# Differential attention: both components' scores into one two-bank tile, one maximum for both, softmax statistics of four heads together

## The chip, the cores and the metric

One core of a Trainium2 chip runs the whole forward pass of a two-layer encoder trunk. The metric is the device time of one execution in microseconds (us); smaller is better. The kernel before takes 2676.36 us (median of three runs, 2675.62 to 2678.28).

## The reference, cut to what matters

Each layer has three head groups that read one input projection: RWKV-7, differential attention, and gated linear attention (GLA). Their outputs meet in one output projection; a mixture of 16 experts follows. The change is in the differential attention (4 heads, two components of 64 dimensions each per head, values of 128; 512 tokens behind 16 meta tokens, so L = 528):

```python
q = rotary(q...) * (B_QK_DIM ** -0.5)      # (B, 4 heads, 2 components, L, 64)
k = rotary(k...)                            # the same shape
def attend(qb):
    s = einsum("bhcqd,bhckd->bhcqk", qb, k)
    pr = softmax(s, axis=-1)                # each component by itself
    w = pr[:, :, 0] - lam * pr[:, :, 1]
    return einsum("bhqk,bhkv->bhqv", w, v)
o_meta = attend(q[:, :, :, :N_META])        # the 16 meta tokens
o_real = lax.map(attend, q_real)            # 4 blocks of 128 queries
o = rms_norm(concatenate(o_meta, o_real), subln_g) * (1.0 - lam_init)
```

## The kernel before

A layer goes through three stages. In the first, the 28 blocks of the input projection (`pj`, L297, float32 as sums of products of a high and a low part) run on TensorE (PE), and GLA and the chunks of the RWKV recurrence are laid between them. `heads` (L763) takes the twelve attention blocks of that projection: for every head it makes `q{h}` and `k{h}`, in which the partitions 0 to 63 hold component 0 and 64 to 127 component 1 (`hr(c)` is that half), after a rotation on VectorE (DVE) and GpSimd (POOL). `k{h}` is stored twice as wide as `q{h}`: a slice of it for each component, in which the other component's half is zero (memset on POOL), so that a product over all 128 rows with `q{h}` gives one component's scores.

In the second stage `attention` (L884) goes through query blocks of 128 in the order 1, 2, meta, 3, 4. For a block PE makes the scores against the 16 meta keys (tile `sm`, L897), ScalarE (ACT) copies them to `smeta` (L900), and DVE takes their maxima `mxm` (L901). Then, for each of four heads and two components: PE makes the scores of 128 queries by 512 keys in one PSUM bank (`S`, L907; `s_tile` has four banks); DVE takes the row maximum (L908) and turns it with `mxm` into the bias (L909); ACT makes the exponentials and their sums (L911), and the same of `smeta` (L913). Per head follow three small statistics on DVE (L915 to L917), the combination of both components (L918 for `e`, L919 for `em`), four transposes on PE into `pt` (L923), their copy `wt` (ACT L927 for heads 0 to 2, DVE L929 for head 3) and four products with the values into `po` (L931). After the heads come the meta weights (`pm`, `wm`, `vM`) and `norm` (L805): `o` and its square on ACT, about fifteen operations on DVE in a chain, four transposes `pf`, and `mxh`/`mxl`, the inputs of the output projection. The meta tokens go through `attend_meta` (L832), all heads in one tile. The last RWKV steps (L587 to L618) and the splitting of the output weights (`wo_h` on ACT L988, `wo_l` on DVE L989, eight each) are laid into this stage as well.

In the third stage the output projection (L1092) runs on PE. Its PSUM tiles take the place of the score tiles, so its first product waits until the last exponential has read its scores. Then the router and the experts follow.

The Tile scheduler fixes, when the kernel is built, the order of instructions on each engine; each engine runs its own list in order and waits where an operand is late. The few lines that matter most:

```python
for c in range(2):
    p = s_tile("S")
    behind(T.matmul(p[:R], qk[0, h][:, qo:qo + R], qk[1, h][:, c, NM:], start=True, stop=True), mark)
    V.tensor_reduce(s_[:, c:c + 1], p[:R], axis=AX.X, op=OP.max)
    V.tensor_scalar(s_[:, c:c + 1], s_[:, c:c + 1], mxm[:R, h, c:c + 1], -0.125, op0=OP.max, op1=OP.mult)
```

## Time and profile before

| | us |
|---|---|
| median of three runs | 2676.36 |
| the profiled execution, its own time | 2676.92 |
| its span in the trace | 2675.1 |
| PE busy | 2498.5 (93%) |
| DVE busy | 2121.9 (79%) |
| ACT busy | 1589.3 (59%) |
| POOL busy | 345.0 (13%) |
| mean granted TensorE clock, share of full speed | 0.951 |

The span goes from the first to the last instruction on the core; 1.8 us of the execution lie around it. Busy shares are means over stages with different limits: the experts take most of the span, and attention about 83 us in each layer. Layer 1's attention stage is from 436.7 us (the first copy of `smeta`) to 519.2 us, layer 2's from 1758 to 1842 us. A share in one of these windows tells about this stage; the shares above do not.

### The profile page before, as it was taken

The page shows a single profiled execution, that of the slowest core. Times are in us where ns is not written, and L with a number is a line of the kernel's source. Part 1 is how long each engine was busy: PE and PEld are TensorE (multiplying, and loading weights), DVE is VectorE, ACT ScalarE, POOL GpSimd, SP SyncE. Part 2 cuts the span into 40 slices and gives each one's busy share as a digit, 9 for nine tenths or more (in the row PEclk, how much of TensorE's full clock was granted, in tenths as well). Part 3 has the DMA queues.
Part 4 walks back from the last instruction along what each step waited for, and adds up shares of the span by engine and source line. Part 5 has one row for each costly group of instructions (what it writes and reads, how often), then busy time and mean ns, then how long its engine had stood idle before and what let it go on. Part 6 is the DMA issues. An engine that isn't in the chain of part 4 may idle for free. (4 is left out here: it accounts for less than half of the span.)

```text
span 2675.1 us, 54651 instructions
## 1 busy us (share of the span) xinstructions
PE 2498.5 (93%) x22106; PEld 2104.4 (79%) x22106; DVE 2121.9 (79%) x3645; ACT 1589.3 (59%) x2337; POOL 345.0 (13%) x503
## 2 busy tenths in 40 slices
PE   7898999897999999999888899999699999999995
PEld 6787876567888888888687787866489898988894
DVE  3557677858999999999735667777699999999995
ACT  4324334515878787888642343354177878787884
POOL 2212331000000000000121133210000000000000
PEclk9878999998999999999988889999899999999998
DMA  4101111158999999999620111012499999999994
GB/s 132 40 33 53 36 35 48 63 198 324 402 400 405 403 403 405 400 408 416 233 84 33 40 45 47 16 68 105 171 387 392 410 399 409 398 409 400 406 420 151
DMA packets 84717, 643.80 MB, mean 241 GB/s; under 512 B 12592, under 2 KB 13040, under 8 KB 35312
## 3 DMA queue, kind: packets, MB, share of 16 engines
q1 hardware_dynamic: 75936, 618.16, 57.8%
q0 software_dynamic: 8528, 22.15, 3.3%
q8 instruction: 173, 2.83, 0.4%
q14 instruction: 80, 0.66, 0.1%
HBM read 617.05 MB, written 19.40 MB: 238 GB/s over the span
## 5 line engine op out<-in xcount | busy, mean ns | idle before, releaser
L1162 DVE TENSOR_TENSOR wl<-w,wh 128x1280 fp32r<-128x1280 f32 (+2 forms) x896 | 1161.4, 1334 | 81.7 <-ACT wh L1161 58.6
L1161 ACT ACTIVATE wh<-w 128x1280 fp32r<-128x1280 f32 (+2 forms) x896 | 1008.4, 1149 | 200.9 <-PE h3b L1215 70.5
L1283 PE MATMUL py<-wh,hh 128*66 128x512 f32 (+1 forms) x768 | 288.6, 376 | 3.2 <-ACT hh L1263 3.2
L1283 PE MATMUL py<-wh,hl 128*66 128x512 f32 (+1 forms) x768 | 287.2, 374 | 0.0
L1283 PE MATMUL py<-wl,hh 128*66 128x512 f32 (+1 forms) x768 | 287.2, 374 | 0.0
L1215 PE MATMUL h1a<-wh,xx 128*66 128x256 f32 x1024 | 243.4, 296 | 0.0
L1215 PE MATMUL h3a<-wh,xx 128*66 128x256 f32 x1024 | 241.5, 294 | 0.0
L1288 POOL DMA_INDIRECT hbuf<-yo,idx x32 | 63.9, 1998 | 1188.2 <-ACT yo L1287 1078.1
L1215 PE MATMUL h1T<-xx,wh 128*128 128x132 f32 x768 | 175.8, 229 | 0.0
L1215 PE MATMUL h3T<-xx,wh 128*128 128x132 f32 x768 | 174.2, 227 | 0.0
L297 PE MATMUL pj<-uh,wh 128*128 128x264 f32 (+1 forms) x896 | 166.3, 314 | 5.4 <-ACT kS L353 5.0
L297 PE MATMUL pj<-ul,wh 128*128 128x264 f32 (+1 forms) x896 | 163.5, 315 | 0.0
L297 PE MATMUL pj<-uh,wl 128*128 128x264 f32 (+1 forms) x896 | 155.3, 303 | 0.0
L1283 PEld LDWEIGHTS py<-wh,hh 128*66 128x66 f32 x768 | 104.8, 136 | 60.9 <-ACT hh L1263 3.5
L1283 PEld LDWEIGHTS py<-wl,hh 128*66 128x66 f32 x768 | 104.7, 136 | 60.7
L1215 PE MATMUL h1a<-wl,xx 128*66 128x256 f32 x512 | 151.8, 296 | 0.0
L1215 PE MATMUL h3a<-wl,xx 128*66 128x256 f32 x512 | 151.1, 295 | 0.0
L1283 PEld LDWEIGHTS py<-wh,hl 128*66 128x66 f32 x768 | 104.8, 136 | 58.1 <-DVE hl L1264 0.7
L1215 PE MATMUL h1T<-xx,wl 128*128 128x66 f32 x768 | 150.1, 195 | 0.0
L1215 PE MATMUL h3T<-xx,wl 128*128 128x66 f32 x768 | 148.9, 194 | 0.0
L1215 PEld LDWEIGHTS h1T<-xx,wh 128*128 128x128 f32 x768 | 148.5, 193 | 0.0
L1215 PEld LDWEIGHTS h3T<-xx,wh 128*128 128x128 f32 x768 | 146.8, 191 | 0.0
(462 smaller groups left out, 6000.9 us busy)
## 6 DMA issues: line engine op xcount, KB each, us to landing
w<-in_e_w SPq DMA_DIRECT2D x384, 1408.0 KB, 15.8
w<-in_w_in SPq DMA_DIRECT2D x56, 512.0 KB, 3.3
wo<-in_w_out SPq DMA_DIRECT2D x16, 512.0 KB, 3.3
h<-hbuf SPq DMA_DIRECT2D x12, 512.0 KB, 5.1
swp<-raw SPq DMA_DIRECT2D x64, 66.0 KB, 2.0
h<-in_x SPq DMA_DIRECT2D x8, 512.0 KB, 7.0
hbuf<-h SPq DMA_DIRECT2D x8, 512.0 KB, 2.9
ubuf<-u POOLq DMA_DIRECT2D x8, 512.0 KB, 7.3
```

The source lines that it names most:

```text
L297: T.matmul(p[:M, c, :HL], ww[:, k, :M], uu[:, k, c * HL:(c + 1) * HL], start=(n == 0), stop=(n == 23))
L1161: A.activation(wh, w[:, lo:hi], AF.Copy)
L1162: sub = V.tensor_sub(wl, w[:, lo:hi], wh.bitcast(F32))
L1215: T.matmul(o_, l_, r_, start=s0, stop=s1)
L1283: T.matmul(py[:CAP, c, d0:d0 + n], x[:, kk, :], ww[:, at0 - lo:at0 - lo + n], start=(kk == 0 and i_ == 0), stop=(kk == FK - 1 and i_ == 2))
L1288: G.indirect_dma_start(out=hbuf[:, :], out_offset=bass.IndirectOffsetOnAxis(ap=idx[:CAP, e:e + 1], axis=0), in_=yo[:CAP], in_offset=None, ...
```

## The change

`k{h}` becomes as wide as `q{h}`: one addition over 128 partitions takes the place of two over 64, and eight zero fills go. A small tile `kM` holds the 16 meta keys of each head and component with zeros in the other half (one memset and eight copies of 64 x 16 on POOL). The scores of a component are a product over its own 64 rows; both components of a head go to the two banks of one tile (`s_tile`: two tiles of two banks, where there were four of one). One maximum over 128 x 2 x 512 and one small operation make both biases. `smeta` is copied with the factor -0.125, so that a minimum takes the place of the maximum. The statistics (sum, reciprocal, ratio, meta weights) are made once per block, for four heads at a time, behind the exponentials of all four heads; then come the four combinations of `e`. The fourth `wt` copy goes from DVE to ACT. In `attend_meta` one product takes the place of two that were added up.

```diff
-        return banks["pool"].tile([128, 512], F32, name=name, tag="s", bufs=4)
+        return banks["pool"].tile([128, 2, 512], F32, name=name, tag="s", bufs=2)
...
+            kM = at.tile([128, 4, 2, NM], F32, name="kM")
+            G.memset(kM, 0.0)
...
-                    if which == 0:
-                        q_ = at.tile([128, L], F32, name=f"q{h}")
-                        V.tensor_add(q_, raw, swp)
-                    else:
-                        q_ = at.tile([128, 2, L], F32, name=f"k{h}")
+                    q_ = at.tile([128, L], F32, name=f"{'qk'[which]}{h}")
+                    V.tensor_add(q_, raw, swp)
+                    if which == 1:
                         for c in range(2):
-                            G.memset(q_[hr(1 - c), c, :], 0.0)
-                            V.tensor_add(q_[hr(c), c, :], raw[hr(c)], swp[hr(c)])
+                            G.tensor_copy(kM[hr(c), h, c, :], q_[hr(c), :NM])
...
-            p, pe = s_tile("S"), s_tile("pe")
+            p2 = s_tile("S")
+            p, pe = p2[:, 0], p2[:, 1]
...
-                for c in range(2):
-                    mm(pe[r, :NM], buf[:, r], qk[1, h][:, c, :NM], start=(c == 0), stop=(c == 1),
-                       tile_position=(0, 32 * h))
-                for c in range(2):
-                    mm(p[r, :], buf[:, r], qk[1, h][:, c, NM:], start=(c == 0), stop=(c == 1),
-                       tile_position=(0, 32 * h))
+                mm(pe[r, :NM], buf[:, r], qk[1, h][:, :NM], start=True, stop=True, tile_position=(0, 32 * h))
+                mm(p[r, :], buf[:, r], qk[1, h][:, NM:], start=True, stop=True, tile_position=(0, 32 * h))
...
-                st = at.tile([128, 4, 12], F32, name="st", bufs=2)
                 e4 = em[qt % 2]
-                pe = s_tile("sm")[:, :128].rearrange("p (h c n) -> p h c n", h=4, c=2)
+                stat = lambda name: at.tile([128, 4, 2], F32, name=name, bufs=2)
+                pe = s_tile("sm")[:, 0, :128].rearrange("p (h c n) -> p h c n", h=4, c=2)
                 for h in range(4):
-                    behind(T.matmul(pe[:R, h], qk[0, h][:, qo:qo + R], qk[1, h][:, :, :NM], start=True, stop=True), mark)
+                    behind(T.matmul(pe[:R, h], qk[0, h][:, qo:qo + R], kM[:, h], start=True, stop=True), mark)
                 sm_ = at.tile([128, 4, 2, NM], F32, name="smeta", bufs=2)
-                mxm = at.tile([128, 4, 2], F32, name="mxm", bufs=2)
-                A.activation(sm_[:R], pe[:R], AF.Copy)
-                V.tensor_reduce(mxm[:R], sm_[:R], axis=AX.X, op=OP.max)
+                low, big_, sums, part, rec = (stat(n_) for n_ in ("low", "big", "sums", "part", "rec"))
+                A.activation(sm_[:R], pe[:R], AF.Copy, scale=-0.125)
+                V.tensor_reduce(low[:R], sm_[:R], axis=AX.X, op=OP.min)
+                es = []
                 for h in range(4):
-                    s_ = st[:R, h]
                     e = wp.tile([128, 1024], F32, name="e", tag=("w", "wh")[h % 2])[:R].rearrange("p (c n) -> p c n", c=2)
+                    p = s_tile("S")
                     for c in range(2):
-                        p = s_tile("S")
-                        behind(T.matmul(p[:R], qk[0, h][:, qo:qo + R], qk[1, h][:, c, NM:], start=True, stop=True), mark)
-                        V.tensor_reduce(s_[:, c:c + 1], p[:R], axis=AX.X, op=OP.max)
-                        V.tensor_scalar(s_[:, c:c + 1], s_[:, c:c + 1], mxm[:R, h, c:c + 1], -0.125,
-                                        op0=OP.max, op1=OP.mult)
-                        A.activation(e[:, c], p[:R], AF.Exp, scale=0.125, bias=s_[:, c:c + 1],
-                                     accum_out=s_[:, 2 + c:3 + c])
-                        A.activation(sm_[:R, h, c], sm_[:R, h, c], AF.Exp, scale=0.125, bias=s_[:, c:c + 1],
-                                     accum_out=s_[:, 8 + c:9 + c])
-                    V.tensor_add(s_[:, 2:4], s_[:, 2:4], s_[:, 8:10])
-                    V.reciprocal(s_[:, 4:6], s_[:, 2:4])
-                    V.scalar_tensor_tensor(s_[:, 6:7], s_[:, 5:6], nlam[:R], s_[:, 2:3], op0=OP.mult, op1=OP.mult)
-                    V.scalar_tensor_tensor(e[:, 0], e[:, 1], s_[:, 6:7], e[:, 0], op0=OP.mult, op1=OP.add)
-                    V.scalar_tensor_tensor(e4[:R, h, :NM], sm_[:R, h, 1], s_[:, 6:7], sm_[:R, h, 0],
-                                           op0=OP.mult, op1=OP.add)
+                        behind(T.matmul(p[:R, c], qk[0, h][hr(c), qo:qo + R], qk[1, h][hr(c), NM:],
+                                        start=True, stop=True), mark)
+                    V.tensor_reduce(big_[:R, h], p[:R], axis=AX.X, op=OP.max)
+                    V.scalar_tensor_tensor(big_[:R, h], big_[:R, h], -0.125, low[:R, h], op0=OP.mult, op1=OP.min)
+                    for c in range(2):
+                        A.activation(e[:, c], p[:R, c], AF.Exp, scale=0.125, bias=big_[:R, h, c:c + 1],
+                                     accum_out=sums[:R, h, c:c + 1])
+                        A.activation(sm_[:R, h, c], sm_[:R, h, c], AF.Exp, scale=-1.0, bias=big_[:R, h, c:c + 1],
+                                     accum_out=part[:R, h, c:c + 1])
+                    es.append(e)
+                V.tensor_add(sums[:R], sums[:R], part[:R])
+                V.reciprocal(rec[:R], sums[:R])
+                ratio = part[:R, :, 0]
+                V.scalar_tensor_tensor(ratio, rec[:R, :, 1], nlam[:R], sums[:R, :, 0], op0=OP.mult, op1=OP.mult)
+                V.tensor_mul(sm_[:R, :, 1], sm_[:R, :, 1], ratio[:, :, None].to_broadcast([R, 4, NM]))
+                V.tensor_add(e4[:R, :, :NM], sm_[:R, :, 1], sm_[:R, :, 0])
+                for h in range(4):
+                    e = es[h]
+                    V.scalar_tensor_tensor(e[:, 0], e[:, 1], part[:R, h, 0:1], e[:, 0], op0=OP.mult, op1=OP.add)
                     pt = sm_tile("pt")
                     for t in range(4):
                         T.transpose(pt[:, t * 128:t * 128 + R], e[:, 0, t * 128:(t + 1) * 128], ident[:R, :R])
                     wt = at.tile([128, 528], F32, name="wt", tag="tb", bufs=4)[:, :512].rearrange("p (t n) -> p t n", t=4)
                     pv4 = pt.rearrange("p (t c) -> p t c", t=4)[:, :, :R]
-                    if h < 3:
-                        A.activation(wt[:, :, :R], pv4, AF.Copy)
-                    else:
-                        V.tensor_copy(wt[:, :, :R], pv4)
+                    A.activation(wt[:, :, :R], pv4, AF.Copy)
...
-                norm(at, po, st[:R, :, 4], qo, R)
+                norm(at, po, rec[:R, :, 0], qo, R)
```

The two lists of instructions differ in three places as follows. Numbers behind a tile's name tell its instance; `x2` is two instructions in a row.

ACT, layer 1, end of block 1 (its last heads' exponentials, `e_5507` and `e_5536`) and the start of block 2 (`smeta_5607`, `e_5611`), before:

```order
L911 ACTIVATE e_5507,st_5439<-S_5514,st_5439 128x512
L913 ACTIVATE smeta_5445,st_5439<-smeta_5445,st_5439 128x16
L900 ACTIVATE smeta_5607<-sm_5602 128x128
L911 ACTIVATE e_5536,st_5439<-S_5537,st_5439 128x512
L617 ACTIVATE mxh_5224<-zf_5308 128x80
L927 ACTIVATE wt_5501<-pt_5496 128x512
...
L913 ACTIVATE smeta_5445,st_5439<-smeta_5445,st_5439 128x16
L911 ACTIVATE e_5536,st_5439<-S_5543,st_5439 128x512
L913 ACTIVATE smeta_5445,st_5439<-smeta_5445,st_5439 128x16
L927 ACTIVATE wt_5530<-pt_5525 128x512
L617 ACTIVATE mxh_5224<-zf_5344 128x128
L911 ACTIVATE e_5611,st_5601<-S_5612,st_5601 128x512
```

The same place after; `e_5480` is block 1's last head and `e_5592` block 2's first:

```order
L908 ACTIVATE e_5480,sums_5445<-S_5481,big_5444 128x512
L910 ACTIVATE smeta_5442,part_5446<-smeta_5442,big_5444 128x16
L896 ACTIVATE smeta_5584<-sm_5579 128x128
L617 ACTIVATE mxh_5222<-zf_5306 128x80
L596 ACTIVATE zf_5378<-Y_2114 128x128
L610 ACTIVATE zf_5342<-pg_5365 128x128
L927 ACTIVATE wt_5501<-pt_5496 128x512
L617 ACTIVATE mxh_5222<-zf_5342 128x128
L927 ACTIVATE wt_5513<-pt_5508 128x512
L610 ACTIVATE zf_5378<-pg_5401 128x128
...
L927 ACTIVATE wt_5537<-pt_5532 128x512
L908 ACTIVATE e_5592,sums_5587<-S_5593,big_5586 128x512
```

Before, the copies `wt` of block 1 stood among its exponentials; now all four stand behind the last of them and ahead of block 2's first.

DVE at the same place, before: the maximum of block 2's first scores (`S_5612`) stands ahead of the combination of block 1's last head (`e_5536`).

```order
L915 TENSOR_TENSOR st_5439<-st_5439 128x2
L908 TENSOR_REDUCE st_5601<-S_5612 128x1
L615 SCALAR_TENSOR_TENSOR zf_5344<-pf_5370,pv_72,zf_5344 128x128
L194 SCALAR_TENSOR_TENSOR rq_u_5388<-rq_u_5388,m2_5379 128x2
L916 RECIPROCAL st_5439<-st_5439 128x2
L909 TENSOR_SCALAR st_5601<-st_5601,mxm_5608 128x1
L195 SCALAR_TENSOR_TENSOR rq_y_5387<-rq_u_5388,rq_y_5387 128x2
L917 SCALAR_TENSOR_TENSOR st_5439<-st_5439,lam_88 128x1
L618 TENSOR_TENSOR mxl_5225<-zf_5344,mxh_5224 128x128
L196 TENSOR_TENSOR rq_u_5388<-rq_y_5387 128x2
L918 SCALAR_TENSOR_TENSOR e_5536<-e_5536,st_5439 128x512
```

After: the ratio (L916), the meta weights (L917, L918) and the four combinations of block 1 (`e_5450` to `e_5480`) stand ahead of block 2's first maximum (`big_5586`).

```order
L916 SCALAR_TENSOR_TENSOR part_5446<-rec_5447,lam_88,sums_5445 128x4
...
L917 TENSOR_TENSOR smeta_5442<-smeta_5442,part_5446 128x4x16
...
L918 TENSOR_TENSOR em1_4915<-smeta_5442 128x4x16
...
L921 SCALAR_TENSOR_TENSOR e_5450<-e_5450,part_5446 128x512
...
L921 SCALAR_TENSOR_TENSOR e_5460<-e_5460,part_5446 128x512
...
L921 SCALAR_TENSOR_TENSOR e_5470<-e_5470,part_5446 128x512
...
L921 SCALAR_TENSOR_TENSOR e_5480<-e_5480,part_5446 128x512
L618 TENSOR_TENSOR mxl_5223<-zf_5342,mxh_5222 128x128
L196 TENSOR_TENSOR rq_u_5386<-rq_y_5385 128x2
L905 TENSOR_REDUCE big_5586<-S_5593 128x2
...
L905 TENSOR_REDUCE big_5586<-S_5603 128x2
...
L906 SCALAR_TENSOR_TENSOR big_5586<-big_5586,low_5585 128x2 x2
```

Block 2's maxima moved behind everything that block 1's statistics have to do.

PE at the end of layer 1's attention, around the first product of the output projection (L1092), before:

```order
L923 MATMUL pt_6113<-cst_66,e_6095 128x128 x4
L1092 MATMUL po_6234<-wo_h_5421,mxh_5224 128x512 x2
L1092 MATMUL po_6234<-wo_h_5421,mxl_5225 128x512 x2
L931 MATMUL po_6026<-vB_4913,wt_6118 128x128 x4
L923 MATMUL pt_6142<-cst_66,e_6124 128x128
L825 MATMUL pf_6019<-cst_66,o_5996 128x128 x4
L923 MATMUL pt_6142<-cst_66,e_6124 128x128 x3
L1092 MATMUL po_6234<-wo_l_5422,mxh_5224 128x512 x2
L1092 MATMUL po_6234<-wo_h_5421,mxh_5224 128x512 x2
L931 MATMUL po_6026<-vB_4913,wt_6147 128x128 x4
L934 MATMUL pm_6153<-cst_66,em0_4916 128x128
...
L937 MATMUL po_6026<-vM_4914,wm_6155 128x512
```

After, where that line is L1090:

```order
L903 MATMUL S_6000<-k3_4907,q3_4637 128x512 x2
L1090 MATMUL po_6143<-wo_h_5419,mxh_5222 128x512 x2
L1090 MATMUL po_6143<-wo_h_5419,mxl_5223 128x512 x2
L824 MATMUL pf_5948<-cst_66,o_5925 128x128 x4
...
L924 MATMUL pt_6015<-cst_66,e_5969 128x128 x4
...
L932 MATMUL pm_6062<-cst_66,em0_4914 128x128
...
L929 MATMUL po_5955<-vB_4911,wt_6020 128x128 x4
L924 MATMUL pt_6027<-cst_66,e_5979 128x128 x4
L924 MATMUL pt_6039<-cst_66,e_5989 128x128 x4
...
L929 MATMUL po_5955<-vB_4911,wt_6032 128x128 x4
L929 MATMUL po_5955<-vB_4911,wt_6044 128x128 x4
L924 MATMUL pt_6051<-cst_66,e_5999 128x128 x4
```

Of block 4's transposes `pt` and value products `po` those of two heads stood ahead of the output projection's first product, and of a third head the transposes; now all four heads' stand behind it.

## Rows read from the trace of the kernel before

**Rows 1.** Windows: stretch, us, then busy us of PE, PEld, DVE, ACT, POOL, clock, DMA

```profile
436.70:519.20 82.50, 73.49 (x421) 43.98 (x421) 75.44 (x288) 56.58 (x181) 5.30 (x10) 0.98 0.16 57
...
1758.00:1842.00 84.00, 74.99 (x444) 45.23 (x444) 75.95 (x287) 56.76 (x181) 6.89 (x11) 0.98 0.16 53
...
300.00:436.00 136.00, 133.33 (x1625) 108.47 (x1624) 89.36 (x213) 46.98 (x108) 37.63 (x79) 1.00 0.13 41
...
485.00:490.00 5.00, 2.40 (x14) 1.90 (x15) 4.31 (x16) 1.93 (x3) 0.00 (x0) 0.79 0.43 148
```

**Rows 2.** Waits in 436.7 to 519.2: who for whom, total us, times, longest

```profile
ACT e L911 <- DVE st L909: 8.2, 6, 2.6
...
PE pt L868 <- DVE mq L865: 3.0, 1, 3.0
```

**Rows 3.** Groups by line, DVE, 436 to 540: xcount, busy us, mean ns, idle before

```profile
L908 DVE TENSOR_REDUCE st<-S 128x1 f32<-128x512 f32 x32 | 21.4, 680 | 0.5 <-PE S L907 0.5
...
L989 DVE TENSOR_TENSOR wo_l<-wo,wo_h 128x1024 fp32r<-128x1024 f32 x8 | 9.7, 1218 | 1.1 <-ACT wo_h L988 1.1
...
L587 DVE TENSOR_REDUCE m<-zf 128x2 f32<-128x128 f32 x4 | 1.1, 275 | 0.0
```

**Rows 4.** Timeline, DVE: start us, duration us, line and operation

```profile
488.77 0.16 DVE L192 TENSOR_SCALAR rq_y<-ms 128x4 int32<-128x4 int32 x1
488.97 0.16 DVE L193 TENSOR_TENSOR rq_u<-rq_y 128x4 f32<-128x4 f32 x1
...
497.70 0.69 DVE L908 TENSOR_REDUCE st<-S 128x1 f32<-128x512 f32 x1
498.31 0.74 DVE L918 SCALAR_TENSOR_TENSOR e<-e,st 128x512 f32<-128x512 f32 x1
498.97 0.23 DVE L919 SCALAR_TENSOR_TENSOR em<-smeta,st 128x16 f32<-128x16 f32 x1
499.12 0.21 DVE L909 TENSOR_SCALAR st<-st,mxm 128x1 f32<-128x1 f32 x1
499.24 1.28 DVE L908 TENSOR_REDUCE st<-S 128x1 f32<-128x512 f32 x2
```

**Rows 5.** Timeline, ACT: same columns, idle before in brackets

```profile
436.72 0.28 ACT L900 ACTIVATE smeta<-sm 128x128 f32<-128x128 f32 x1 [1.02 <-PE sm L897]
...
439.19 0.69 ACT L911 ACTIVATE e<-S,st 128x512 f32<-128x512 f32 x1 [0.28 <-DVE st L909]
...
451.20 0.69 ACT L911 ACTIVATE e<-S,st 128x512 f32<-128x512 f32 x1 [1.14 <-DVE st L909]
...
494.06 0.68 ACT L911 ACTIVATE e<-S,st 128x512 f32<-128x512 f32 x1
...
495.01 0.68 ACT L911 ACTIVATE e<-S,st 128x512 f32<-128x512 f32 x1
...
518.37 0.71 ACT L911 ACTIVATE e<-S,st 128x512 f32<-128x512 f32 x1
```

**Rows 6.** Timeline, PE: same columns

```profile
422.47 1.01 PE L297 MATMUL pj<-uh,wl 128*128 128x264 f32 x7
...
461.37 1.12 PE L907 MATMUL S<-k,q 128*128 128x512 f32 x2
462.43 0.45 PE L614 MATMUL pf<-cst,zf 64*64 64x64 f32 x8
...
471.51 1.92 PE L833 MATMUL S<-k,mq 128*32 128x512 f32 x10
...
503.50 0.60 PE L923 MATMUL pt<-cst,e 128*128 128x128 f32 x4
503.94 1.88 PE L907 MATMUL S<-k,q 128*128 128x512 f32 x4
505.66 1.05 PE L931 MATMUL po<-vB,wt 128*128 128x128 f32 x8
...
519.61 0.71 PE L1092 MATMUL po<-wo_h,mxh 128*128 128x512 f32 x2
```

More of the change, by code (lines that the diff above doesn't have):

```diff
@@ L802, in heads @@
                 A.activation(vB[:, :, h * 128:(h + 1) * 128], pt.rearrange("p (t c) -> p t c", t=4), AF.Copy)
-            return qk, vB, vM, em, mark
+            return qk, kM, vB, vM, em, mark
         def norm(at, po, i4, qo, R):
@@ L830, in norm, with attend_meta @@
                                    mh[:, 2:6, qo:qo + R].bitcast(F32), op0=OP.mult, op1=OP.subtract)
-        def attend_meta(at, po, qk, vB, vM, em, mark):
+        def attend_meta(at, po, qk, kM, vB, vM, em, mark):
             mm = lambda *x, **k: behind(T.matmul(*x, **k), mark)
             buf = wp.tile([128, 1024], F32, name="mq", tag="wl")
-            p, pe = s_tile("S"), s_tile("pe")
+            p2 = s_tile("S")
+            p, pe = p2[:, 0], p2[:, 1]
             G.memset(buf[:, :128], 0.0)
@@ L882, in attend_meta, with attention @@
             T.matmul(po[:NM, :], wm, vM, start=False, stop=True)
-        def attention(at, qk, vB, vM, em, mark):
-            hd = (qk, vB, vM, em, mark)
+        def attention(at, qk, kM, vB, vM, em, mark):
+            hd = (qk, kM, vB, vM, em, mark)
             for qt in (1, 2, 0, 3, 4):
```

## The prediction

> **What bounds the kernel now.** I read the busy shares by window first, since the shares of the whole span belong to the experts. In layer 1's attention (82.5 us) DVE is busy for 75.4, ACT for 56.6, PE for 73.5 [rows 1]; layer 2's window reads the same. PE's figure says less than it seems to: a score product is busy for about .6, but four of them follow at .43 each (503.94 to 505.66) [rows 6]. Next the waits: the largest of ACT in this stretch is 8.2 us for the biases of DVE [rows 2]. So **DVE is the limit here**, and what ends the stage is the last exponential, 518.37 to about 519.1, because the first output product, at 519.61, takes over the PSUM banks of the scores [rows 5, 6]. I call that point the gate: 82.5 us behind the first smeta copy at 436.72. Ahead of attention it is another engine: from 300 to 436 PE is busy for 133.3 of 136 and DVE for 89 [rows 1]. Behind the gate PE is the limit as well.
>
> The first exponentials of the blocks 1 to 3 begin 2.5, 14.5 and 57.3 us after the smeta copy [rows 5]; between the second and the third lie the meta tokens, the last RWKV steps and eight wo_l of 1.2 us each [rows 3].
>
> **The change part by part**, first for one layer.
>
> *Ahead of attention.* Of the eight half-height additions for k, four go, and eight fills on POOL; nine small POOL operations come. DVE has 46 of 136 us to spare there and POOL nearly 100 [rows 1], so I cost this at nothing; were that cover gone, four additions of roughly .7 (one pass over 528 elements; a 512-element pass is .68 [rows 3]) would be 2.8 us gained. The order has a loss, though: 29 fewer projection products are laid ahead of the last RWKV chunk's pu step (L559) and stand in a row ahead of the first meta scores instead. Seven of them take 1.01 us, .14 each [rows 6], so at most 29 x .14 = 4.1 us later, if PE stood idle where they are missing, and nothing if it did not. PE has 2.7 idle us in the whole window; I take **+1.0**, from 0 to +4.1.
>
> *DVE's work per block.* A 512-element reduction is followed by the next operation after .61 us (497.70 to 498.31), a small operation after .12 (499.12 to 499.24), and after .20 if it needs the one before it (488.77 to 488.97); a combination of e takes .66 [rows 4]. A reduction over 1024 elements isn't in the trace. From 128 to 512 elements the mean goes from 275 to 680 ns [rows 3], 1.05 ns an element, so .60 + 512 x 1.05 = 1.14; two single ones, 1.20, bound it from above. I take 1.14. Then a block saves
> - 4 x (1.20 - 1.14) = .24 on maxima, and 8 x .12 - 4 x .13 = .44 on biases;
> - the statistics: 12 small operations of about .12 and four em of .15 (498.97 to 499.12), 2.04, become a chain of five at .20, 1.0: 1.04, or about .7 since some of the small ones overlap with their neighbours;
> - the wt copy that moves to ACT: .6.
>
> That is 2.3, with overlap 2.0: **8 us a layer**. ACT has 26 us to spare for the copy. Besides, of block 4 all four combinations and the statistics (2.6 + 1.0) now stand behind the gate, where before about 1.8 of it stood: another 1.8 leave the stretch. DVE's work ahead of the gate is 75.4 - 8 - 1.8 = 65.6.
>
> *The waits.* Now the other side. Before, the statistics of one head ran under the exponentials of the next, and the next block's first maximum stood ahead of the old block's last combination. After, a block has two phases. ACT makes eight pairs of exponentials at .95 each (494.06 to 495.01 [rows 5]), 7.6 us. Only then DVE has the sums: five small operations (1.0), four combinations (2.6), two double maxima and their biases (2.5) come before the next block's first exponential, 6.2 us in all. That is 13.8 a block, against DVE's 14.8 before (four heads at 2.5, norm 3.7, the rest 1.0), if the other engine always found something to do. I walked the new lists of ACT, DVE and PE row by row with these pitches:
> - block 1's first exponential at 3.6 (before 2.5): it needs a pair of scores (+.43) and 1.14 + .13 instead of .61 + .12;
> - block 2's at 23.4: DVE makes four double maxima and biases (5.1), the rest of RWKV (about 9), 1.0 and 2.6, and waits 2.1 of the 19.8;
> - block 3's at 43.0: 5.1, 1.0 and 2.6, two wo_l (2.4), a norm (3.7) and the meta tokens (about 4), 18.8 of 19.6;
> - block 4's at 63.6: 5.1, six wo_l (7.2), a norm (3.7), block 2's wm and the like make 17; ACT stands for 3 us before the meta tokens' copy of po, a row that lies ahead of block 4's first exponential;
> - the last one ends at 76.8: 7.6, and 5.6 of waits for maxima, which share DVE with block 3's statistics and combinations.
>
> So 65.6 of work and 11.2 of waits, where there were 7.1: the gate comes at 76.8 instead of 82.5, **-5.7**. If no wait is added it is -9.8, at best -12 if ACT's pauses fill too; if the waits double once more, it is about 0.
>
> *Behind the gate.* PE, the limit there, still has four sets of transposes of .44 (503.50 to 503.94), four of value products of at most 1.05, meta weights (.5) and two pf (.9): 7.4 to 7.8 us, where there were a transposition, two sets of products and the same rest, 4.4 [rows 6]. That work isn't new, but it slips past the point from which PE counts: **+3.4** (from 0, if it falls into pauses, to 3.4).
>
> *PE.* A component's product over 64 rows costs as many columns as over 128. I take .43 for a pair, i.e. that the two halves run at the same time, and no price for switching between 64 and 128 rows. Column tiles do overlap here: ten products with 32 columns of queries take 1.92 [rows 6], .19 each. Row halves aren't in the trace. A pair that doesn't overlap costs .86, and a change of form shows in one place: a pair of scores at 461.37 is followed by 64*64 products after 1.06 instead of .86, .2 for the change. The Trainium skill, TensorEngine Tiling (Array Packing), Key Properties, says that tiles run independently, but that changing the tiling mode drains TensorE. The first half speaks for .43 a pair, the second for a price at each change, and the place above agrees with a drain; the rival below prices it from rows.
>
> *Sum.* -5.7 + 3.4 + 1.0 = -1.3 a layer, both layers alike (the lists are the same there), **-2.6**. From the profiled execution, 2676.92, that is 2674.3; its time lies .56 over the median of the runs, so I forecast **2673.8**.
>
> **The rivals.**
>
> *The new waits are covered* (faster). The walk may be too strict: then DVE's saved work shows nearly whole, the gate comes 9 earlier, and -9 + 3.4 + 1.0 = -4.6 a layer gives 2676.4 - 9.2 = 2667.2. For it: DVE is busy in 91% of the stretch. Against it: what filled ACT's and DVE's waits, the neighbouring head, is now tied to the end of the block.
>
> *Pairs don't overlap* (slower; the change doesn't do what it says on PE). A pair costs .86 and a switch on either side .2 each, .8 more than forecast. That counts only where a maximum waits for its pair: with two score tiles instead of four banks the third pair of a block can't start before the first head's exponentials, and the first pair of a block opens it; about five such places a layer, +4, so +2.7 a layer, 2681.8. It decides from about four places on.
>
> *The clock falls* (slower). In a phase in which only DVE works, PE stands. Before, PE waited 3.0 us for one step of the meta tokens [rows 2], and in 485 to 490, in which that wait ends, the granted clock was .79 [rows 1], a mean of 2.4 and 1.2 GHz; the rest of attention was near 1.00. The new phases leave PE with nothing for up to 4 us in each block. At 1.2 GHz the products on the path (two pairs, transposes and value products, some 3.8 us a block) take twice as long; if that holds in half of them, it costs 3.8 x 4 / 2 = 7.6 a layer: 2676.4 - 2.6 + 15.2 = 2689. Against it: PE's pauses of about 3 us gave .79 in one window only.
>
> **How the numbers follow.** Forecast .40 (its own range 2669 to 2680, from the bounds of waits and start); covered waits .36; no overlap .14; clock .08; something else .02. The gate at -12 with the rest as forecast gives -7.6 a layer, 2661, the low end; doubled waits (0 + 3.4 + 1.0) give 2685, the high end, which takes in the pairs that don't overlap and leaves the clock out. Of this kernel's time a measurement can tell .2%, 5.4 us. Faster by more: the covered waits and the lower end of the forecast, .42. Slower by more: the clock, most of the no-overlap rival, the upper end of the forecast, .20. Within: .38.
>
> **What would show it.** A 1024-element maximum with a mean near 1.2 us incl. its latency, and a pair of scores .43 after the one before it, would show the prices; pairs at .86 the second rival. The gate should come 76 to 78 us behind the first smeta copy, with DVE busy for about 66 of them. Waits of ACT for the biases should be at the block starts, three or four of about 5 us (partly filled with copies), waits of DVE for ACT's last sums before each block's statistics. Wrong would be: a gate at 73 or earlier (covered waits), a granted clock under .9 in the stage (the clock), a first meta copy more than 2 us later, or PE idle in the output projection because block 4's inputs come late.

## The result, and the profile after

The changed kernel takes 2705.01 us (median of four runs, 2700.13 to 2708.67), the kernel before 2677.32 beside it: a ratio of 1.0104, with a 95% interval of 1.0082 to 1.0127. One of the four runs of the kernel before took 3468.32 us and is left out of the ratio. The changed kernel is slower by some 28 us, where 2.6 us less were forecast, and lies outside the range of 2661 to 2685.

The page of the profiled execution after (its time is 2708.67): the span, busy time by engine, and the granted clock in 40 slices.

```profile
span 2706.8 us, 54472 instructions
...
PE 2512.4 (93%) x22074; PEld 2116.5 (78%) x22074; DVE 2099.9 (78%) x3477; ACT 1594.4 (59%) x2345; POOL 338.1 (12%) x505
...
PEclk9877998797999999999988889988989999999998
```

DVE has 22 us less to do in the whole span, and the span is 32 us longer. In the page's row of clocks the seventh and the eighth slice, in which layer 1's attention lies (437 to 530 us, 67.7 a slice), read 8 and 7, where both were 9 before; in layer 2 the 27th and the 28th go from 9 to 8.

The stage is easiest to compare from its first meta score to the end of the output projection, in one window. Columns are as in [rows 1]: length, busy us of PE, PEld, DVE, ACT and POOL, granted clock, DMA. Before, layer 1, the same cut at the first product of the output projection (the gate), and layer 2:

```profile
435.60:590.30 154.70, 145.23 (x807) 98.22 (x803) 114.25 (x433) 68.12 (x206) 8.07 (x13) 0.99 0.27 98
435.60:519.60 84.00, 74.99 (x437) 45.48 (x434) 76.34 (x293) 56.93 (x183) 6.40 (x10) 0.98 0.16 58
519.60:590.30 70.70, 70.24 (x373) 52.74 (x371) 37.91 (x142) 11.19 (x23) 1.67 (x3) 1.00 0.39 146
...
1758.70:1913.70 155.00, 145.51 (x807) 98.33 (x803) 114.26 (x433) 68.11 (x206) 8.12 (x13) 0.99 0.27 96
```

After, both layers, and layer 1 cut at the gate:

```profile
437.60:607.60 170.00, 152.16 (x809) 104.02 (x807) 107.63 (x352) 71.57 (x212) 7.57 (x12) 0.87 0.24 89
1775.60:1945.60 170.00, 152.18 (x809) 104.08 (x807) 107.64 (x352) 71.64 (x212) 7.61 (x12) 0.87 0.23 88
...
437.60:529.30 91.70, 76.34 (x412) 46.67 (x410) 65.92 (x196) 56.45 (x177) 5.90 (x9) 0.80 0.12 42
529.30:607.60 78.30, 75.82 (x398) 57.35 (x398) 41.71 (x157) 15.13 (x36) 1.67 (x3) 0.96 0.39 145
```

Both layers lose 15.0 to 15.3 us, together 30.3 of the 31.7 between the spans. 7.7 of them stand ahead of the gate (91.7 us; 84.0 before, counted from the first meta score) and 7.6 behind it (78.3; 70.7 before). Ahead of the gate DVE is busy for 65.9 us, as forecast (65.6), but now it is idle for 25.8 us of the 91.7. And the clock is .80 there, where it was .98.

What a low clock does is seen in PE's timeline of layer 1 after (start us, us, line, operation, records; the clock levels are 2.4 and 1.2 GHz):

```profile
438.51 1.13 PE L903 MATMUL S<-k,q 64*128 64x512 f32 x4
439.57 0.80 PE L614 MATMUL pf<-cst,zf 64*64 64x64 f32 x20
...
454.21 2.07 PE L903 MATMUL S<-k,q 64*128 64x512 f32 x2
456.21 0.79 PE L609 MATMUL pg<-sg,pw 128*128 128x128 f32 x2
...
461.26 1.97 PE L924 MATMUL pt<-cst,e 128*128 128x128 f32 x8
...
466.09 1.04 PE L924 MATMUL pt<-cst,e 128*128 128x128 f32 x8
...
469.93 1.12 PE L903 MATMUL S<-k,q 64*128 64x512 f32 x2
```

Eight transposes take 1.97 at 461.26 and 1.04 at 466.09. At 438.51 a pair of score products (four records) is followed after 1.06, and at 469.93 half a pair (two records) after 1.05 (by a product at 470.98); at 454.21 half a pair takes 2.00. The waits of ACT in the same stretch, longest first (total us, times, longest), show where it arrives:

```profile
ACT wt L927 <- PE pt L924: 11.0, 6, 5.1
ACT o L808 <- PE po L935: 5.6, 2, 3.9
```

ACT's largest wait is no longer for the biases of DVE [rows 2], it is for PE's transposes. The combinations of DVE stand ahead of these transposes, so not all of it need be the clock's.

### The profile page after: what moved, and what is told of

It is laid out like the page before. It is cut to its first block, busy times and chain, and to the rows that moved or that the text cites. A ratio compares the mean times of both kernels' runs of the same rounds, so it can differ in the third digit from the quotient of the medians.

```text
span 2706.8 us, 54472 instructions
## 1 busy us (share of the span) xinstructions
PE 2512.4 (93%) x22074; PEld 2116.5 (78%) x22074; DVE 2099.9 (78%) x3477; ACT 1594.4 (59%) x2345; POOL 338.1 (12%) x505
## 5 line engine op out<-in xcount | busy, mean ns | idle before, releaser
L1213 PE MATMUL h1a<-wl,xx 128*66 128x256 f32 x512 | 151.6, 296 | 0.0
L1213 PE MATMUL h3a<-wl,xx 128*66 128x256 f32 x512 | 151.3, 295 | 0.0
```

The lines of the kernel that those rows point to most:

```text
L1213: T.matmul(o_, l_, r_, start=s0, stop=s1)
```

## The experiments

The theories: **A**, grouping the statistics leaves PE without work between bursts, and the clock falls for that. **B**, the products on 64 rows bring the clock down. **C**, the phases cost by their waits, and the clock matters little. A fourth, **D** (the clock is not what costs, the order of the instructions is), came with e5. To tell them apart the three parts of the change (64 rows, one maximum for both components, statistics of four heads) were taken one by one. The kernels that start from before write the bias and the statistics in after's form (a minimum of negated scores, tiles of their own), which leaves DVE's count as it was: 433 operations in the stage of layer 1 before, 433 in e9. e4 and e5 also have after's narrow `k{h}` and `kM`.

One table first. *Stage* is the window from the first meta score to the end of the output projection in layer 1 (or as noted), *low* is the time at 1.2 GHz that its clock means: twice the share that is missing to 1.00, times its length (the clock is read to .01, so *low* is good to 1.5 or 2 us). The last column takes .39 us off for each us of low clock, a price that e1, e10 and e11 give below; for the other kernels the column is an estimate.

| run | rows | maximum | statistics | time, ratio to before | stage | clock | low | stage less .39 x low |
|---|---|---|---|---|---|---|---|---|
| before | 128 | each | head | 1 | 154.7 | .99 | 3 | 153.5 |
| after | 64 | both | four heads | 1.0104 | 170.0 | .87 | 44 | 152.8 |
| e1 | 64 | both | head | 1.0029 | 154.3 | .98 | 6 | 151.9 |
| e2 | 128 | both | four heads | 1.0085 | 165.9 | .95 | 17 | 159.4 |
| e3 | 128 | both | head | 1.0003 | 155.7 | .98 | 6 | 153.3 |
| e4 | 64 | each | head | 1.0051 | 164.6 | .91 | 30 | 153.0 |
| e5 | 64, twice | each | head | 1.0317 | 204.3 | .84 | 65 | 178.8 |
| e6 | after, with added products | | | 1.0113 | 172.7 | .90 | 35 | 159.2 |
| e7 | e2, last block per head | | | 1.0032 | 160.4 | .97 | 10 | 156.7 |
| e8 | after, last block per head | | | 1.0076 | 170.1 | .87 | 44 | 152.9 |
| e9 | 128, twice | each | head | 1.0103 | 171.4 | 1.00 | 0 | 171.4 |
| e12 | 128 | both | head, fourth copy on ACT | .9953 | 151.3 | .99 | 3 | 150.1 |
| e13 | 128, and small ones on 64 | each | head | 1.0021 | 158.0 | 1.00 | 0 | 158.0 |
| e14 | 64 | both | head, fourth copy on ACT | .9985 | 168.7 | .87 | 44 | 151.6 |

**e1**: the changed kernel with the statistics per head (and the fourth copy back on DVE).

```diff
-                V.tensor_add(sums[:R], sums[:R], part[:R])          # and four more, behind all four heads
+                    V.tensor_add(sums[:R, h], sums[:R, h], part[:R, h])   # and four more, in each head
...
-                    A.activation(wt[:, :, :R], pv4, AF.Copy)
+                    if h < 3:
+                        A.activation(wt[:, :, :R], pv4, AF.Copy)
+                    else:
+                        V.tensor_copy(wt[:, :, :R], pv4)
```

> The changed kernel with the statistics taken back to one head at a time (64-row products and the one maximum for both components kept; the fourth wt copy back on DVE). Theory A (grouping leaves PE without work between bursts, the clock falls to 1.2 GHz and PE's pieces take twice as long): hardly any slow products, time 2665 to 2680. Theory B (the 64-row products themselves bring the clock down, half of the rows being idle): slow products stay, 2695 to 2705. Theory C (the phases cost by their waits, the clock follows and matters little): 2665 to 2680, like A.

Measured: 1.0029 (1.0009 to 1.005), and an unexpected scatter: ten runs between 2674.75 and 2701.12, where 19 of the kernel before lay between 2674.77 and 2686.09. The median, 2687.52, is in the range of none of the theories, so e10 and e11 came back to it.

**e2**: the changed kernel with its scores on 128 zero-padded rows, as before the change (with `k{h}` twice as wide again, its zero fills, and no `kM`).

```diff
-                        behind(T.matmul(p[:R, c], qk[0, h][hr(c), qo:qo + R], qk[1, h][hr(c), NM:],
+                        behind(T.matmul(p[:R, c], qk[0, h][:, qo:qo + R], qk[1, h][:, c, NM:],
```

> The changed kernel with the scores back on 128 zero-padded rows (one maximum and grouped statistics kept), so that PE has about 14 us more work a layer and no change between 64 and 128 rows. Theory A: PE is fuller, part of the slow products goes, 2685 to 2698. Theory B: no slow products, 2670 to 2680. Theory C: the phases are the same, 2700 to 2710.

Measured: 1.0085 (1.0067 to 1.0103). Of the low clock, 44 us, 17 are left, but the ratio went down by .0019 only, some 5 us. The windows up to the gate and behind it, and the wait of PE that is largest behind it:

```profile
435.90:520.70 84.80, 71.88 (x408) 43.93 (x406) 64.53 (x194) 54.49 (x173) 5.88 (x9) 0.94 0.13 45
520.70:601.80 81.10, 75.79 (x399) 57.86 (x398) 43.24 (x158) 16.10 (x38) 1.67 (x3) 0.96 0.39 140
...
PE pf L825 <- DVE rec L937: 4.8, 1, 4.8
```

The gate comes at 84.8 (before 84.0), though DVE has some 12 us less to do ahead of it (64.5 for 76.3); then PE stands for 4.8 us at the transposes of block 3's norm, while output products stand behind them in its list. Grouping thus costs by itself, also where most of the clock is kept, and 64 rows aren't the whole cause. The time, 2703.32, lies in C's range; A is met in direction but not in size, and B's 2670 to 2680 is missed.

**e3** (before with the one maximum) and **e4** (before with 64 rows):

```diff
 e3
-        return banks["pool"].tile([128, 512], F32, name=name, tag="s", bufs=4)
+        return banks["pool"].tile([128, 2, 512], F32, name=name, tag="s", bufs=2)
-                        V.tensor_reduce(s_[:, c:c + 1], p[:R], axis=AX.X, op=OP.max)
+                    V.tensor_reduce(big_[:R, h], p[:R], axis=AX.X, op=OP.max)
 e4
-                        behind(T.matmul(p[:R], qk[0, h][:, qo:qo + R], qk[1, h][:, c, NM:], start=True, stop=True), mark)
+                        behind(T.matmul(p[:R], qk[0, h][hr(c), qo:qo + R], qk[1, h][hr(c), NM:],
+                                        start=True, stop=True), mark)
```

> The kernel before with one two-bank tile and one maximum for both components only (128 rows, statistics per head). All theories: DVE saves about .7 us a block on maxima and biases; two tiles instead of four banks may add waits: 2670 to 2680. Near 2700 would mean that the two-tile ring itself is the cause, which none of them holds.

> The kernel before with 64-row products only (single banks, a maximum for each component, statistics per head). The halves of a pair may run at the same time, PE has up to 14 us less work a layer. Theory A: PE stays in step with DVE, few slow products, 2672 to 2685. Theory B: slow products in much of attention, 2690 to 2705. Theory C: 2672 to 2680.

Measured: e3 1.0003 (.9992 to 1.0013), no change, as all expected (its 2681.73 us lie 1.7 over the stated range, with the kernel before at 2681.52 beside it). e4 1.0051 (1.0031 to 1.007), 2695.34, with 30 us of low clock and no grouping at all: B's range, and against A and C. Its stage in layer 1:

```profile
432.80:597.40 164.60, 151.55 (x809) 100.44 (x807) 112.78 (x432) 69.31 (x208) 7.52 (x12) 0.91 0.25 92
```

**e5 and e9**, a pair: every score product issued twice, on 64 rows in e5 and on 128 in e9.

```diff
+                        for again in range(2):
+                            behind(T.matmul(p[:R], ...
```

> e4 (64-row products only, 1.005 of before, 30.7 us of low clock in each layer's attention and output projection, where the kernel before has 3.4) with every score product issued twice into the same place, so that PE is as long at work for a pair as with 128 rows; nothing else is added. Theory A (the clock falls because PE has too little to do between its waits): the low clock goes back under 10 us a layer, and the time falls although PE has 14 us more work a layer, to 0.998 to 1.001 of before. Theory B (products on 64 rows are what the clock falls for, however long they take): low clock stays at 25 to 40 us, time at 1.005 to 1.010. Theory D (the clock is not what costs in e4; the order of the instructions is): low clock may go, time stays at 1.004 or more.

> The partner of e5: the kernel before (128 zero-padded rows, a maximum for each component, statistics per head) with every score product issued twice. The number of products and the columns of each are those of e5, only the rows differ (128 in place of 64). e5 was 1.032 of before, with 64.9 us of low clock in each layer's attention and output projection, though PE was busy 125 of 134 us up to the gate. Theory B (products on 64 rows bring the clock down, however many there are): low clock under 10 us here, gate below 120 us and 1.005 to 1.022 of before, from the added products alone. Theory A' (any PE-bound stretch of this form is granted the low clock, or the added products alone explain e5): low clock over 40 us and 1.03 again.

Measured: e5 1.0317 (1.0273 to 1.036), e9 1.0103 (1.0069 to 1.0136). The windows up to the gate, e5 and then e9:

```profile
438.90:573.10 134.20, 125.44 (x516) 67.27 (x514) 82.53 (x298) 61.01 (x187) 6.45 (x9) 0.77 0.09 29
```

```profile
437.50:539.70 102.20, 100.72 (x512) 57.85 (x509) 81.32 (x296) 59.39 (x185) 5.80 (x9) 1.00 0.12 41
```

PE is busy for 125.4 of 134.2 us in e5 and yet at .77 (61.7 us at 1.2 GHz); in e9, 100.7 of 102.2 at 1.00. The number of products and their columns are the same, only the rows differ, and the clock falls on 64. It is so in every run: the mean clock of the whole span is .931 to .939 in the four of e5, .952 and .956 in the two of e9. PE has some 7 us more of pauses in e5, but these alone don't explain it: the kernel before has 9.0 us of them in 84.0, at .98, and within e5 the clock stays low where PE's list shows no wait, from 453.04 to 479.75:

```profile
453.04 2.07 PE L918 MATMUL S<-k,q 64*128 64x512 f32 x2
...
477.13 2.07 PE L918 MATMUL S<-k,q 64*128 64x512 f32 x2
```

So A falls in the form that PE only needs more to do: filling PE up with 64-row products made it worse. B's direction stands, but e5 lies outside every range that was stated, B's too (25 to 40 us of low clock and 1.005 to 1.010 were expected; 65 and 1.0317 came). e9 lies in B's (1.005 to 1.022).

**e6**: the changed kernel with twelve products a layer that nobody reads.

```diff
                     pt = sm_tile("pt")
+                    if qt != 4:
+                        T.matmul(pt, ident, vB[:, 0, :], start=True, stop=True)
```

> The changed kernel with one product of 128 x 512 that nobody reads ahead of each set of transposes in blocks 1 to 3 (into the tile that the transposes then overwrite, so it can run while PE waits for the combination of e): 12 x .86 = 10 us more PE work a layer. Theory A: the low clock falls from 44 us a layer to under 25 and the time falls by 5 us or more, to below 1.0085 of before. Theory C (waits): the time stays at 1.010 or rises by up to the added work, 1.010 to 1.017.

Measured: 1.0113 (1.0091 to 1.0134), low clock 35 us instead of 44. A asked for a low clock under 25 and a time below 1.0085, and has neither; the time lies in C's range. But 9 us less low clock are worth some 4 (an estimate by the price of .39), and the added work, 7.5 us of PE's time, can hide them: e6 decides little.

**e7 and e8**: e2, and the changed kernel, with the last query block's statistics per head.

```diff
+                g = 1 if qt == 4 else 4       # heads in a group of statistics
```

> e2 (128 rows, one maximum, grouped statistics, 1.0085 of before) with the statistics of the last query block, and of it alone, taken per head. In e2 the gate came .5 us later than before, but the output projection behind it took 81.1 us instead of 70.7. If the loss of grouping sits at the end of the stage (all of block 4's transposes and value products behind the gate, PE's list standing at the transposes of block 3's norm for 4.8 us): the output projection is back at 71 to 73 and the time at 0.998 to 1.002. If the phases of every block cost: the gate moves later instead and the time stays above 1.005.

> The changed kernel with the statistics of the last query block alone taken per head. If the loss sits at the end of the stage: output projection back from 78.4 to 71 to 74 us, the gate unchanged at about 92, so 1.004 to 1.007. If it is the clock by the thin PE work of all blocks (theory A): low clock still 30 us or more a layer, 1.007 to 1.010.

Measured: e7 1.0032 (1.0017 to 1.0047), e8 1.0076 (1.0058 to 1.0095). The output projections are back, 70.8 and 71.0 us (e2 81.1, after 78.3), but the gate moved later, to 89.6 and 99.1. e7's time lies between its two ranges. e2 less e12 (below), which differs from it in grouping alone, is .0132; .0053 of it come back in e7, so some two fifths sit at the end of the stage and the rest in the phases of the other blocks. In e8, with 64 rows, the clock is .87 again and the expectation for the end of the stage was missed: the loss moved ahead of the gate with the low clock, as the other one said.

**e10 and e11**: e1's kernel again, to have more traces of one list.

> The kernel of e1 once more (64 rows, one maximum, statistics per head): ten runs of it lay between 2674.75 and 2701.12, and the one whose trace there is was the fastest, with 6.8 us of low clock in layer 1 and 13.7 in layer 2. The list of instructions is the same, so if the low clock is what costs, this trace lies on one line with the first: for every further us of low clock .3 to .5 us of time, as between the two layers of e1 (6.9 us more, 1.9 to 2.3 us longer) and of e8 (6.9 us more, 3.7 us less). If the low clock costs little, time and low clock are unrelated.

> The same as e10, a third trace of the same list: its time less that of e1's trace should be .3 to .5 of the difference of their low clock in the two attention stages and output projections (theory of the clock), or unrelated to it.

Measured: 2691.49 and 2713.96 us; e1's trace was 2674.75. The stage in both layers, e1, e10, e11:

```profile
431.00:585.30 154.30, 142.05 (x809) 95.39 (x807) 111.95 (x400) 68.91 (x208) 7.49 (x12) 0.98 0.27 98
1753.70:1910.10 156.40, 144.45 (x809) 97.43 (x807) 112.21 (x400) 69.28 (x208) 7.54 (x12) 0.96 0.26 95
```

```profile
435.70:606.90 171.20, 160.05 (x809) 104.63 (x807) 112.71 (x400) 69.30 (x208) 7.47 (x12) 0.86 0.24 89
1775.10:1927.90 152.80, 140.47 (x809) 94.15 (x807) 111.97 (x400) 68.95 (x208) 7.57 (x12) 0.99 0.27 97
```

```profile
432.60:607.40 174.80, 163.91 (x809) 107.88 (x807) 112.98 (x401) 69.55 (x208) 7.46 (x12) 0.83 0.24 87
1774.70:1949.20 174.50, 163.32 (x809) 107.24 (x807) 112.98 (x401) 69.52 (x208) 7.50 (x12) 0.83 0.23 85
```

Six times the same instructions in the same order, DVE busy for 112 to 113 us each time, and lengths from 152.8 to 174.8 in the order of their clocks, .99 to .83. From 3.1 us of low clock to 59.4 the stage grows by 22.0: **.39 us for each us at 1.2 GHz**, within the .3 to .5 expected. By the whole time it is .39 for e11 and .52 for e10, since e10's time also grew by 3.4 us outside the two stages. D is answered by this: the order is the same each time, and the time is not. The Trainium skill, TensorE: Matmul & The Clock Gate, Terms, puts the penalty at the throttled time times the share of the clock that is missing, which would be .5 here, an estimate. The trace is a fifth below that; PE was idle for 11 to 12 us of each stage anyway, which may be why. Where the two layers of e10 part, PE's timeline reads, layer 1 and then layer 2:

```profile
443.30 0.45 PE L609 MATMUL pg<-sg,pw 128*128 128x80 f32 x2
443.68 1.60 PE L918 MATMUL S<-k,q 64*128 64x512 f32 x2
445.21 1.11 PE L902 MATMUL pt<-cst,e 128*128 128x128 f32 x4
446.26 2.07 PE L918 MATMUL S<-k,q 64*128 64x512 f32 x2
...
1782.66 0.45 PE L609 MATMUL pg<-sg,pw 128*128 128x80 f32 x2
1783.04 1.12 PE L918 MATMUL S<-k,q 64*128 64x512 f32 x2
1784.09 0.66 PE L902 MATMUL pt<-cst,e 128*128 128x128 f32 x4
1784.68 1.12 PE L918 MATMUL S<-k,q 64*128 64x512 f32 x2
```

The products at 443.68 and 1783.04 begin 7.97 and 7.96 us behind the first meta score of their layers; up to there the two timelines agree, and from there one runs at half speed. The clock falls first and the delays follow, so it is a cause here and not a companion. What PE had done in the stage until then was the same: a list with 64-row scores may keep its clock or lose it. The Trainium skill, TensorE: Matmul & The Clock Gate, Part 1 (The HAM clock gate), says that the number of slow products at the start of a kernel varies from run to run. The traces agree that one list varies, here in the middle of the kernel and between two layers of one run.

**e12**: e3 with the fourth copy of a block on ACT.

```diff
-                    if h < 3:
+                    if h < 4:
```

> e3 (128 rows, one maximum, statistics per head; 1.0003 of before) with the fourth wt copy of a block on ACT instead of DVE, the last part of the change that was not run by itself. DVE has .6 us a block less: if DVE still bounds the stage and no wait takes its place, 2 us a layer, 0.9985; if ACT's row ahead of the next block's exponentials takes it back, 1.000 to 1.001.

Measured: **.9953 (.9936 to .997)**, 2668.39 us, faster than both kernels and by more than expected (.9985). Layer 1, the part of it behind the gate, and layer 2:

```profile
433.60:584.90 151.30, 141.93 (x807) 98.48 (x803) 110.75 (x398) 70.40 (x210) 7.48 (x12) 0.99 0.28 100
513.90:584.90 71.00, 70.41 (x372) 52.68 (x370) 37.76 (x142) 11.83 (x25) 1.67 (x3) 1.00 0.38 141
...
1753.90:1903.60 149.70, 140.31 (x807) 97.61 (x803) 110.63 (x397) 70.31 (x210) 7.53 (x12) 1.00 0.27 99
```

Against e3's stage of 155.7 and DVE's 113.3 there, 2.4 us of copies went, the clock kept up (.99 and 1.00), and by the last column of the table the stage is 3 us shorter. So DVE's time was indeed worth having, once nothing took PE's clock. With layer 2 (156.0 in e3, at .98) the two stages are 10.7 us shorter for 4.8 us of copies; the better clock is a part of the rest, and how much of it stays open.

**e13 and e14**: what of 64 rows it is, and whether it holds on the fastest list.

```diff
 e13 (before, with a small product on 64 rows ahead of each on 128)
+                        behind(T.matmul(p[:R, :16], qk[0, h][hr(c), qo:qo + R], qk[1, h][hr(c), c, NM:NM + 16],
+                                        start=True, stop=True), mark)
 e14 (e12 with 64-row scores)
-                        behind(T.matmul(p[:R, c], qk[0, h][:, qo:qo + R], qk[1, h][:, c, NM:],
+                        behind(T.matmul(p[:R, c], qk[0, h][hr(c), qo:qo + R], qk[1, h][hr(c), NM:],
```

> The kernel before with a product on 64 rows and 16 columns ahead of every score product on 128 rows (into the place that the latter overwrites): the changes between the two forms are those of 64-row scores or more, the work on half of the rows is next to nothing. If the changes of form bring the clock down: low clock of 20 us or more in a layer's attention and output projection, 1.005 or more of before. If the work on half of the rows does: low clock under 10 us, 1.000 to 1.006 (64 changes of .2 us at most, where they lie on the path).

> e12 (0.9953 of before, 0 to 3 us of low clock a layer) with 64-row scores and nothing else: the rows alone, on the best list so far. PE has up to 11 us less to do a layer. If products on 64 rows bring the clock down: stretches of low clock of 7 to 58 us in a layer and a time that scatters, 0.998 to 1.010. If e12's list keeps the clock up anyway: 0.993 to 0.996.

Measured: e13 1.0021 (.998 to 1.0063), both layers at a clock of 1.00; e14 .9985 (.9942 to 1.0028), four runs between 2666.59 and 2691.62. The stage of e13, layer 1, and of e14, layers 1 and 2:

```profile
433.20:591.20 158.00, 155.97 (x871) 106.76 (x867) 113.21 (x434) 69.20 (x206) 7.94 (x12) 1.00 0.26 96
```

```profile
438.10:606.80 168.70, 159.65 (x809) 104.60 (x807) 110.48 (x396) 71.79 (x212) 7.47 (x12) 0.87 0.24 90
1775.20:1927.00 151.80, 142.73 (x809) 96.18 (x807) 110.43 (x396) 71.44 (x212) 7.57 (x12) 0.98 0.27 98
```

The changes between the forms alone don't bring the clock down; the work on half of the rows does. PE is busy for 99% of e13's stage, though, so changes of form beside pauses were not tried. In e14 the same list runs at .87 in one layer and .98 in the other, 16.9 us apart (.45 for each us of low clock). At their best the 64 rows are worth nothing that can be measured (2666.59 against e12's 2666.39), at their worst 25 us.

With e14 four kernels form a square. All have one maximum and the fourth copy on ACT; they differ in rows and grouping alone. Each ratio is to the kernel before in the runs beside it:

| | statistics per head | of four heads |
|---|---|---|
| 128 rows | e12: .9953 | e2: 1.0085 |
| 64 rows | e14: .9985 | after: 1.0104 |

**Grouping is the larger part of the loss**: .0132 on 128 rows and .0119 on 64, 32 to 35 us, beyond the intervals. The 64 rows cost .0032 and .0019 here, which the intervals don't tell from nothing; e4 shows .0051 of them by themselves. On 128 rows grouping lengthens the stage of layer 1 from 151.3 to 165.9 us, 10.1 of it behind the gate (71.0 to 81.1), and takes the low clock from 3 to 17. On 64 rows it goes with a low clock that comes every time: .87 in both layers of after (its four runs have a mean clock of .935 to .938), .87 and .98 in e14 (.942 to .952).

## Why the prediction was wrong, point by point

- **What bounds the stage: right at 2.4 GHz, and only there.** DVE's work ahead of the gate was forecast at 65.6 us and is 65.9. In e12, with DVE's work cut and the clock kept, the kernel is faster. But where the statistics are grouped, DVE's work no longer sets the time: e2 has some 12 us less of it than before, at a clock of .94, and its gate isn't earlier.
- **The price of a double maximum: right.** DVE's timeline after (start us, us) has the next operation 1.13 us behind it, against 1.14:

```profile
463.52 1.22 DVE L905 TENSOR_REDUCE big<-S 128x2 f32<-128x1024 f32 x1
464.65 0.15 DVE L197 TENSOR_TENSOR rq_u<-rq_u,m 128x2 f32<-128x2 f32 x1
```

- **The waits: the term that failed.** The gate came 90.7 us behind the smeta copy, not 76.8; 11.2 us of waits were forecast ahead of it and some 25 measured. The walk gave the first exponentials at 3.6, 23.4, 43.0 and 63.6 behind the smeta copy; they came at 3.2, 29.1, 53.2 and 75.5. Every price in the walk was one of a row at 2.4 GHz, while the stage ran at .80 up to the gate. By the price of .39 its 36.7 us of low clock are 14.3, and 91.7 would be 77.4, where the walk has 77.8 (76.8, and 1.0 from the first meta score to the smeta copy). The whole stage would be 152.8, .7 shorter than before's 153.5, where -2.3 was forecast (-5.7 and +3.4). That is an estimate: the price is e1's, and no run of the changed kernel kept its clock. e4 and e8 come out alike with it (153.0 and 152.9), but e2 and e7, grouped on 128 rows, at 159.4 and 156.7. There the waits cost time that the clock doesn't explain.
- **The step at fault is the rival "the clock falls"**, given a chance of .08 and 7.6 us a layer and left out of the sum and the range. It happened, by the sign that the prediction names (a granted clock under .9 in the stage: .80), and the stage lost 15.3. Its size came from PE's pieces on the path in half of the blocks; in fact 44 us of each stage ran at 1.2 GHz, and what waited for PE was late (ACT stood for 11.0 us before transposes, a part of it DVE's). Its cause was looked for in PE's pauses alone. These do count, as the square shows: grouping takes the low clock from 3 to 17 us on 128 rows, and on 64 rows makes it come every time. e4, e5 and e9 show the other cause: 64-row products, which I had weighed for their overlap and their changes of form and not for the clock. That the forecast saw grouping as a gain for DVE, with 4.1 us of added waits, is the same error: it costs 32 to 35 us.
- **PE's own prices: misread by a factor of two.** The four records at 503.94 [rows 6] are two products, not four: a product of float32 leaves two records (so the ten with 32 columns at 471.51 are five). By line, before:

```profile
L907 PE MATMUL S<-k,q x128: 592/592/697, 436.5 to 1838.5; 128*128 128x512 f32 x128
```

The two layers have 64 score products. So one costs .86, two in a row 1.72, and a pair on 64 rows 1.06 (438.51 to 439.57 above), the change of form included. The halves do run at the same time: the rival "pairs don't overlap" is refuted, and PE's gain was larger than forecast. The Trainium skill, TensorEngine Tiling (Array Packing), Key Properties, has it that tiles work in parallel and that a change of mode drains the engine. The trace agrees with the first; the .2 us a change fit the second without showing a drain. Neither decided the time.
- **Behind the gate: +3.4 forecast, +7.6 measured.** e4 happens to have a list with about as much of the last block behind the gate (396 records of PE; after 398, before 373), and its clock is 1.00 there:

```profile
523.10:597.40 74.30, 73.87 (x396) 55.50 (x394) 40.86 (x154) 13.38 (x27) 1.67 (x3) 1.00 0.40 152
```

That is 3.6 us more than before's 70.7, so the term was about right. For the other 4.0 us there are the clock of .96 (2.4 us by the price of .39, an estimate) and a wait of 2.0 us for the norm of block 3.
- **Ahead of attention: +1.0 forecast, not settled.** The first meta score came 2.0 us later in layer 1; with one list, in e1, e10 and e11, it lay anywhere from 431.0 to 435.7.

## What to carry to other kernels

A price list taken at one clock holds at that clock only: where a change takes rows or work from TensorE beside another bound, price the stage at half the clock as a case of its own, with everything that waits for PE. Work taken off the engine that bounds a stage is worth nothing if the new order ties the engines to each other: grouping saved DVE 3 us of the stage (e12 110.8, e2 107.8) and lengthened it by 14.6. Zero-padding to 128 rows looked like waste and cost nothing here; the gain lay in the plain part, in moving a .6 us copy off the engine that bounds the stage. And a kernel whose runs begin to scatter is telling that its clock hangs on chance: take several traces of one list before believing one.

## What the runs showed of the hardware

Score products of 512 columns on 64 of 128 rows can bring TensorE's clock to 1.2 GHz though PE is busy for 93% of the stretch (e5, .77), while as many on 128 rows keep 2.4 GHz (e9, 1.00), and so does a list with small 64-row products of 16 columns between those on 128 (e13, 1.00). Statistics of four heads together go with a lower clock too, also on 128 rows (e2 .95, e12 .99). With an unchanged list of 64-row products the clock may or may not fall: one kernel took from 2674.75 to 2713.96 us, its stage from 152.8 to 174.8. How the chip decides stays open: within one trace (e10) it went either way after the same 8 us of work in the stage. Two 64-row products on the two halves of the rows run at the same time: a pair takes 1.06 us with a change of form, one of them 1.05, two full-row products 1.72.
